# GpSimd's sums, splits and squares move to VectorE and ScalarE, and GLA's neighbour scores become products, in an encoder trunk on one core

## The chip, the core and the metric

The kernel runs on one core of a Trainium2 chip. The metric is the device time of one execution in microseconds, as the median of several runs. TensorE does the matrix products, VectorE and ScalarE the elementwise work, GpSimd some of it, and SyncE issues all DMAs.

## The reference

Two layers over 1024 tokens of 1024 features, all in float32. Each has a token mixer and a squared-ReLU MLP, with an RMS norm ahead of and behind each of them:

```python
h = x
for l in range(DEPTH):
    mixed = hybrid_mixer(rmsnorm(h, norm_pre_mix[l]), ...)   # mLSTM | GLA | retention
    h = h + rmsnorm(mixed, norm_post_mix[l])
    ff = squared_relu_mlp(rmsnorm(h, norm_pre_ffn[l]), w_ff1[l], w_ff2[l])
    h = h + rmsnorm(ff, norm_post_ffn[l])

def rmsnorm(x, g):
    return x * rsqrt(mean(x * x, axis=-1) + EPS) * g

def squared_relu_mlp(u, w1, w2):
    return square(relu(u @ w1)) @ w2
```

Gated linear attention (GLA) is one of the three mixers. Within a chunk, token i looks at token j <= i of the same head:

```python
b = cumsum(log_decay)                       # per head and feature d
scores[i, j] = sum_d q[i, d] * k[j, d] * exp(b[i, d] - b[j, d])
```

## The kernel before

The tokens are cut into two halves of 512, and a half's activations lie with features on the partitions, as 8 tiles of 128x512. A dense product is done in float32 precision by three passes (`mm3`, L268 to L270): weights and activations are split into a high part (a cast on ScalarE, `h_`/`uh_`) and the rest (a subtraction on VectorE, `l_`/`ul_`; `split`, L276 and L277). `wslot` (L257 to L264) loads and splits the weights. A group of 256 output columns (`fm_group`) has two PSUM banks, `d_...`, from a pool of two, and `evac` empties each. So a bank that is emptied late holds up the group behind it.

Beside the dense groups run generators: a mixer in quarters of 256 tokens, or a norm. `tick`, which `fm_group` calls after each block of 12 matmuls on a bank, takes the next step of them, and what a step issues stands in the program there. The framework's scheduler then sets the order on each engine, by priorities (`tc.high_priority`), and each engine works through its queue in order. All DMAs are in SyncE's queue.

The norms: `square_sum` (L345) squares 8 tiles on ScalarE (`sq_`, L353) and adds them into `ss` (L354): tiles 1 to 4 on GpSimd, 5 to 7 on VectorE. A product with a matrix of ones sums over the partitions (`nps_`), `rstd_end` makes the factor, and `pre_norm_end` (L362) scales and splits the tiles; the splits of tiles 2 and 5 are GpSimd's. `post_norm_end` (L383) does the norm behind a block: L390 multiplies by the factor and L391 applies the gain and adds the residual. There are 6 places with `square_sum`. `out_proj` (L838) copies each output tile from PSUM on ScalarE (L846), squares it and adds it to `sso`: tiles 1 to 6 on GpSimd, tile 7 on VectorE (`block_sq`, L858).

The MLP: a hidden tile is `r` = relu (ScalarE, L873), its square's high part `hi` = square(r) cast (ScalarE, L876), r*r in full (GpSimd, L877), and the rest r*r - hi (VectorE, L878). There are 128 such tiles. The second product is added up in `f` (VectorE, L897), from PSUM.

GLA's scores in `mixer`: the decay between two tokens is split at the border of a block of s tokens, for s = 64, 32, ... 1. At each of the 7 levels `level_operands` builds `Qg` and `Kg` (VectorE and an exp on ScalarE: `e`), a matrix product gives `gs`, and `copy_predicated` (L631) writes its entries, by a mask, into `Pg`. The diagonal, i = j, is a product q*k summed over each head's 32 features by a product with the selector `hsel` (`dd`), which GpSimd spreads over a diagonal (`Pg`, L619). The mixer runs 8 times.

Of the kernel before, what the change touches and what calls it, by code (L numbers as in the profile page):

```python
# [10 lines left out]
F32 = mybir.dt.float32  # L11
F32R = mybir.dt.float32r
I32 = mybir.dt.int32
U8 = mybir.dt.uint8
AF = mybir.ActivationFunctionType
ALU = mybir.AluOpType
# [3 lines left out]
P = 128  # L20
# [7 lines left out]
QT = 256  # L28
EPS = 1e-6
DFF = 4 * D  # L30
LEVELS = (64, 32, 16, 8, 4, 2, 1)
VW = 516
BIG = 1e30

# [12 lines left out]
def hybrid_trunk(ctx, tc, a, out):  # L47
# [153 lines left out]

    cb = cp.tile([P, 768], F32, tag="c_b", name="c_b")
    lmask, dm, gin = cb[:, 0:128], cb[:, 128:640], cb[:, 640:768]
    lvm = cp.tile([P, len(LEVELS) * 64], U8, tag="lvm", name="lvm")

    def load_masks():
        dma(out=cb, in_=a["c_b"])
        lvf = m1.tile([P, len(LEVELS) * 64], F32, tag="mqk", name="lvf")
        dma(out=lvf, in_=a["c_lvm"])
        V.tensor_copy(out=lvm, in_=lvf)  # L210

# [60 lines left out]
    def split(src, name, eng=V):  # L272

        hi = up.tile([P, TH], F32R, tag="uh", name=f"uh_{name}")
        lo = up.tile([P, TH], F32R, tag="ul", name=f"ul_{name}")
        S.copy(out=hi, in_=src)  # L276
        eng.tensor_tensor(out=lo, in0=src, in1=hi.bitcast(F32), op=ALU.subtract)  # L277
        return hi, lo
# [66 lines left out]
    def square_sum(tiles, name):  # L345
        ss = None
        for kt in range(KT):
            if kt == 0:
                ss = np_.tile([P, TH], F32, tag="ss", name=f"ss_{name}", bufs=3)
                S.activation(out=ss, in_=tiles[0], func=AF.Square)  # L350
            else:
                sq = np_.tile([P, TH], F32, tag="nt", name=f"sq_{name}_{kt}", bufs=3)
                S.activation(out=sq, in_=tiles[kt], func=AF.Square)  # L353
                (V if kt >= KT - 3 else G).tensor_tensor(out=ss, in0=ss, in1=sq, op=ALU.add)  # L354
        return ss

    def pre_norm(h, l, key, name):
# [4 lines left out]
    def pre_norm_end(h, r, l, key, name):  # L362
        u = []
        for kt in range(KT):
            w = np_.tile([P, TH], F32, tag="nt", name=f"w_{name}_{kt}", bufs=3)
            V.scalar_tensor_tensor(out=w, in0=h[kt], scalar=pcol(l, key, kt), in1=r, op0=ALU.mult, op1=ALU.mult)
            u.append(split(w, f"{name}_{kt}", G if kt in (2, 5) else V))
        return u

    def post_norm(half, acc, ss, l, key, name, store):  # L370
# [118 lines left out]
    def mixer(pj, prev, q):  # L489
# [117 lines left out]

        qk = m1.tile([P, QT], F32, tag="ge", name=f"qk{nm}", bufs=2)
        V.tensor_tensor(out=qk, in0=gq, in1=gk, op=ALU.mult)
        ready = level_operands(0, LEVELS[0])  # L610
        yield
        ps = psc.tile([P, 512], F32, tag="sc", name=f"dd{nm}")
        for c in range(2):
            PE.matmul(ps[:, 4 * c:4 * c + 4], qk[:, c * P:(c + 1) * P], hsel, start=True, stop=True)
        dd = m1.tile([P, 8], F32, tag="dd", name=f"dd{nm}")
        V.tensor_copy(out=dd, in_=ps[:, :8])
        Pg = m1.tile([P, 2, 4, P], F32, tag="Pg", name=f"Pg{nm}")
        Pg8 = Pg.rearrange("p c h t -> p (c h) t")
        G.tensor_tensor(out=Pg8, in0=ident.unsqueeze(1).to_broadcast([P, 8, P]), in1=dd.unsqueeze(2).to_broadcast([P, 8, P]), op=ALU.mult)  # L619
        yield  # L620
        for li, s in enumerate(LEVELS):
            qb, kb = Qg[li % 2], Kg[li % 2]
            if li + 1 < len(LEVELS):
                ready = level_operands(li + 1, LEVELS[li + 1])
            ps = psc.tile([P, 512], F32, tag="sc", name=f"gs{nm}_{s}")
            for c in range(2):
                mm = PE.matmul(ps[:, c * 256:(c + 1) * 256], kb[:, c * P:(c + 1) * P], qb[:, :, c * 64:(c + 1) * 64], start=True, stop=True)
                if c == 0 and li + 1 < len(LEVELS):
                    behind(mm, ready)
            n2 = 64 // s  # L630
            V.copy_predicated(out=Pg.rearrange("p c h (n w s) -> p (c h) n w s", w=2, s=s)[:, :, :, 1, :],  # L631
                              mask=lvm[:, li * 64:(li + 1) * 64].rearrange("p (n s) -> p n s", s=s).unsqueeze(1).to_broadcast([P, 8, n2, s]),
                              data=ps.rearrange("p (k n s) -> p k n s", k=8, s=s))
            yield
# [203 lines left out]
    def out_proj(pj, y, tiles=None):  # L838
        l, n = pj.l, pj.n
        acc = []  # L840
        ss = np_.tile([P, TH], F32, tag="ss", name=f"sso{n}", bufs=3)
        for g in range(4):
            def ev(m, ps):
                kt = 2 * g + m
                t = tiles[kt] if tiles else accp.tile([P, TH], F32, tag="acc", name=f"o{n}_{kt}")
                S.copy(out=t, in_=ps)  # L846
                acc.append(t)
                return lambda: block_sq(ss, t, tp.tile([P, TH], F32, tag="tmp", name=f"bo{n}_{kt}"), kt, G if kt < KT - 1 else V)
            fm_group(a["w_out"][l][:, 256 * g:256 * (g + 1)], y, ev, f"out{n}_{g}")
        return acc, ss  # L850

    def block_sq(ss, src, sq, kt, eng=V):

        if kt == 0:
            S.activation(out=ss, in_=src, func=AF.Square)
        else:
            S.activation(out=sq, in_=src, func=AF.Square)
            eng.tensor_tensor(out=ss, in0=ss, in1=sq, op=ALU.add)  # L858


    def ffn_steps(l, half, u, late=False, done=None):

        n = f"{l}{half}"
        st = {"acc": [None] * KT, "ss": None}
        hid = {}
        NCH = DFF // 512

        def f1(c, g):
            def ev(m, ps):
                f = 2 * g + m  # L870
                nm = f"hid{n}_{c}_{f}"
                r = tp.tile([P, TH], F32, tag="tmp", name=f"r_{nm}")
                S.activation(out=r, in_=ps, func=AF.Relu)  # L873
                hi = up.tile([P, TH], F32R, tag="uh", name=f"h_{nm}")
                lo = up.tile([P, TH], F32R, tag="ul", name=f"l_{nm}")
                S.activation(out=hi, in_=r, func=AF.Square)  # L876
                G.tensor_tensor(out=r, in0=r, in1=r, op=ALU.mult)  # L877
                V.tensor_tensor(out=lo, in0=r, in1=hi.bitcast(F32), op=ALU.subtract)  # L878
                hid[(c, f)] = (hi, lo)
            col = 512 * c + 256 * g  # L880
            fm_group(a["w_ff1"][l][:, col:col + 256], u, ev, f"f1{n}_{c}_{g}")

        def scratch(kt):
            if not late:
                return np_.tile([P, TH], F32, tag="nt", name=f"bf{n}_{kt}", bufs=3)
            return tp.tile([P, TH], F32, tag="tmp", name=f"bf{n}_{kt}")

        def f2(c, g):
            def ev(m, ps):
                kt = 2 * g + m  # L890
                if c == 0:
                    t = accp.tile([P, TH], F32, tag="acc", name=f"f{n}_{kt}")
                    V.tensor_copy(out=t, in_=ps)
                    st["acc"][kt] = t
                else:
                    t = st["acc"][kt]
                    V.tensor_tensor(out=t, in0=t, in1=ps, op=ALU.add)  # L897
                if c == NCH - 1:
                    if kt == 0:
                        st["ss"] = np_.tile([P, TH], F32, tag="ss", name=f"ssf{n}", bufs=3)  # L900
                    def rest():
                        sq = scratch(kt)
                        if done and kt == KT - 1:
                            S.activation(out=sq, in_=t, func=AF.Square)
                            st["last"] = sq
                        else:
                            block_sq(st["ss"], t, sq, kt)
                        if done:
                            done(kt, t)
                    return rest  # L910
            fm_group(a["w_ff2"][l][512 * c:512 * (c + 1), 256 * g:256 * (g + 1)], [hid[(c, f)] for f in range(4)], ev, f"f2{n}_{c}_{g}")

        steps = [lambda c=c, g=g: f1(c, g) for c in range(2) for g in range(2)]
        for c in range(NCH):
            steps += [lambda c=c, g=g: f2(c, g) for g in range(4)]
            if c + 2 < NCH:
                steps += [lambda c=c, g=g: f1(c + 2, g) for g in range(2)]
        return steps, st
# [201 lines left out]
        return done, finish  # L1120

    AFTER, NEXT = 2, 10
    PARTS = 81


    main, gates = in_groups(pj[0, 0], u0, rn0, sl0)
# [79 lines left out]
def _constants():  # L1206
# [11 lines left out]
    hsel = p[:, None] // 32 == np.arange(4)[None, :]  # L1218
    c = {"c_a": np.concatenate([np.eye(P), freq, hsel, gout], 1).astype(np.float32),
         "c_b": np.concatenate([lmask, dm.reshape(P, 4 * P), gin], 1).astype(np.float32)}  # L1220
    m = np.zeros((P, len(LEVELS), 64), np.float32)
    for li, s in enumerate(LEVELS):
        x = np.arange(64)
        blk = x // s
        m[:, li, :] = (p[:, None] // s == 2 * blk[None, :])
# [30 lines left out]
```

## Time and profile before

| | |
|---|---|
| time, median of 3 runs | 2483.89 us (2482.72 to 2485.12) |
| the profiled execution: time, span | 2483.34 us, 2481.6 us |
| TensorE busy | 2413.4 us (97%) |
| VectorE busy | 1572.0 us (63%), 2800 instructions |
| ScalarE busy | 1065.6 us (43%), 2050 instructions |
| GpSimd busy | 299.7 us (12%), 253 instructions |
| mean granted TensorE clock | 0.995 |

The span is the time from the first to the last instruction of the profiled execution; its own time is longer by what lies around it. Busy shares are means over the whole span. A wait is idle time of an engine that ended with the instruction named.

### The profile page before, as it was taken

The page shows a single profiled execution, that of the slowest core. Times are in us where ns is not written, and L with a number is a line of the kernel's source. Part 1 is how long each engine was busy: PE and PEld are TensorE (multiplying, and loading weights), DVE is VectorE, ACT ScalarE, POOL GpSimd, SP SyncE. Part 2 cuts the span into 40 slices and gives each one's busy share as a digit, 9 for nine tenths or more (in the row PEclk, how much of TensorE's full clock was granted, in tenths as well). Part 3 has the DMA queues.
Part 4 walks back from the last instruction along what each step waited for, and adds up shares of the span by engine and source line. Part 5 has one row for each costly group of instructions (what it writes and reads, how often), then busy time and mean ns, then how long its engine had stood idle before and what let it go on. Part 6 is the DMA issues. An engine that isn't in the chain of part 4 may idle for free. (4 is left out here: it accounts for less than half of the span.)

```text
span 2481.6 us, 31329 instructions
## 1 busy us (share of the span) xinstructions
PE 2413.4 (97%) x11436; PEld 1981.8 (80%) x11436; DVE 1572.0 (63%) x2800; ACT 1065.6 (43%) x2050; POOL 299.7 (12%) x253
## 2 busy tenths in 40 slices
PE   8999998999999989999999999999999999999998
PEld 7778887788788778888788878888888887888886
DVE  5888757756755685856755576776865538634434
ACT  6666344433333454633423344553433344423233
POOL 0000011101111120010110022010110012111010
PEclk9999999999999999999999999999999999999999
DMA  8645454333334355523423445543323433433331
GB/s 252 204 132 170 143 174 153 105 95 116 103 104 151 125 170 172 151 91 108 127 78 117 157 144 165 178 129 109 117 87 93 138 126 111 145 94 94 94 95 67
DMA packets 324246, 321.61 MB, mean 130 GB/s; under 512 B 15434, under 2 KB 292476, under 8 KB 324092
## 3 DMA queue, kind: packets, MB, share of 16 engines
q1 hardware_dynamic: 324092, 319.61, 41.7%
q8 instruction: 90, 1.47, 0.3%
q14 instruction: 64, 0.52, 0.1%
HBM read 263.92 MB, written 55.64 MB: 129 GB/s over the span
## 5 line engine op out<-in xcount | busy, mean ns | idle before, releaser
L263 ACT CAST h_f<-r_f 128x1024 fp32r<-128x1024 f32 x256 | 267.7, 1046 | 558.1 <-PE d_f L270 553.1
L264 DVE TENSOR_TENSOR l_f<-r_f,h_f 128x1024 fp32r<-128x1024 f32 x256 | 319.3, 1247 | 181.3 <-ACT h_f L263 178.3
L268 PE MATMUL d_f<-h_hid,l_f 128*128 128x512 f32 x1024 | 417.9, 408 | 8.6 <-DVE f L897 7.1
L268 PE MATMUL d_f<-uh_uf,l_f 128*128 128x512 f32 x1024 | 417.0, 407 | 4.3 <-ACT uh_uf L276 4.3
L269 PE MATMUL d_f<-ul_uf,h_f 128*128 128x512 f32 x1024 | 406.5, 397 | 0.1
L269 PE MATMUL d_f<-l_hid,h_f 128*128 128x512 f32 x1024 | 406.4, 397 | 0.0
L270 PE MATMUL d_f<-uh_uf,h_f 128*128 128x512 f32 x1024 | 403.3, 394 | 0.0
L270 PE MATMUL d_f<-h_hid,h_f 128*128 128x512 f32 x1024 | 402.9, 393 | 0.0
L877 POOL TENSOR_TENSOR r_hid<-r_hid 128x512 f32<-128x512 f32 x128 | 163.9, 1280 | 1127.5 <-ACT h_hid L876 1127.5
L897 DVE TENSOR_TENSOR f<-f,d_f 128x512 f32<-128x512 f32 x224 | 153.4, 685 | 140.1 <-PE d_f L270 139.6
L268 PEld LDWEIGHTS d_f<-h_hid,l_f 128*128 128x128 f32 x1024 | 193.6, 189 | 58.6 <-DVE f L897 9.4
L268 PEld LDWEIGHTS d_f<-uh_uf,l_f 128*128 128x128 f32 x1024 | 193.7, 189 | 49.7 <-ACT uh_uf L276 4.5
L270 PEld LDWEIGHTS d_f<-uh_uf,h_f 128*128 128x128 f32 x1024 | 192.8, 188 | 44.4
L270 PEld LDWEIGHTS d_f<-h_hid,h_f 128*128 128x128 f32 x1024 | 192.7, 188 | 43.9
L269 PEld LDWEIGHTS d_f<-ul_uf,h_f 128*128 128x128 f32 x1024 | 193.1, 189 | 42.2 <-issue 1.2
L269 PEld LDWEIGHTS d_f<-l_hid,h_f 128*128 128x128 f32 x1024 | 192.9, 188 | 42.5 <-issue 2.4
L878 DVE TENSOR_TENSOR l_hid<-r_hid,h_hid 128x512 fp32r<-128x512 f32 x128 | 89.4, 698 | 163.4 <-POOL r_hid L877 162.5
L264 DVE TENSOR_TENSOR l_in<-r_in,h_in 128x1024 fp32r<-128x1024 f32 (+2 forms) x96 | 122.0, 1271 | 74.4 <-ACT h_in L263 74.3
L873 ACT ACTIVATE r_hid<-d_f 128x512 f32<-128x512 f32 x128 | 76.5, 598 | 195.4 <-PE d_f L270 195.3
L263 ACT CAST h_in<-r_in 128x1024 fp32r<-128x1024 f32 (+2 forms) x96 | 101.4, 1056 | 47.7 <-PE d_in L270 39.2
L269 PE MATMUL d_in<-ul_u,h_in 128*128 128x512 f32 x256 | 101.9, 398 | 4.6 <-DVE ul_u L277 4.6
L268 PE MATMUL d_in<-uh_x,l_in 128*128 128x512 f32 x256 | 104.9, 410 | 1.1 <-DVE px L446 0.9
(394 smaller groups left out, 4261.3 us busy)
## 6 DMA issues: line engine op xcount, KB each, us to landing
r_f<-in_w_ff_dram SPq DMA_DIRECT2D x256, 512.0 KB, 3.7
r_in<-in_w_in_dram SPq DMA_DIRECT2D x80, 512.0 KB, 4.0
r_out<-in_w_out_dram SPq DMA_DIRECT2D x32, 512.0 KB, 3.5
pv<-pv SPq DMA_DIRECT2D x64, 128.0 KB, 2.4
pf<-px SPq DMA_DIRECT2D x32, 256.0 KB, 4.2
vt<-pv SPq DMA_DIRECT2D x32, 256.0 KB, 3.9
pg<-gz_g SPq DMA_DIRECT2D x32, 256.0 KB, 2.0
gt<-pg SPq DMA_DIRECT2D x32, 256.0 KB, 4.6
```

The lines of the kernel that those rows point to most:

```text
L263: S.copy(out=hi[:, :, :n], in_=raw[:, :, :n])
L264: V.tensor_tensor(out=lo[:, :, :n], in0=raw[:, :, :n], in1=hi[:, :, :n].bitcast(F32), op=ALU.subtract)
L268: nc.tensor.matmul(ps, al, bh, start=start, stop=False)
L269: nc.tensor.matmul(ps, ah, bl, start=False, stop=False)
L270: dense[0] = nc.tensor.matmul(ps, ah, bh, start=False, stop=stop)
L873: S.activation(out=r, in_=ps, func=AF.Relu)
L877: G.tensor_tensor(out=r, in0=r, in1=r, op=ALU.mult)
L878: V.tensor_tensor(out=lo, in0=r, in1=hi.bitcast(F32), op=ALU.subtract)
L897: V.tensor_tensor(out=t, in0=t, in1=ps, op=ALU.add)
```

## The change

Five things change.

1. `square_sum`: all sums are on VectorE (24 more over the 6 places).
2. `pre_norm_end`: the splits of tiles 2 and 5 are on VectorE (12 more).
3. `out_proj`: the sums of tiles 1 to 6 are on VectorE (24 more).
4. MLP: ScalarE squares `r` in place and casts it to `hi`; GpSimd has no part in it.
5. GLA: level s = 1 goes. Its entries, the score of each odd token with its left neighbour, are computed as products q*k*exp(b[i]-b[j]) in `nb` (VectorE, an exp on ScalarE), summed over a head's features by two more products with `hsel` into the tile of `dd`, and written by a `copy_predicated` over GpSimd's diagonal. One step of the generator fewer per quarter: `PARTS`, which sets the pace of the mixer, is 79 for 81.

```diff
-LEVELS = (64, 32, 16, 8, 4, 2, 1)
+LEVELS = (64, 32, 16, 8, 4, 2)
...
                 S.activation(out=sq, in_=tiles[kt], func=AF.Square)
-                (V if kt >= KT - 3 else G).tensor_tensor(out=ss, in0=ss, in1=sq, op=ALU.add)
+                V.tensor_tensor(out=ss, in0=ss, in1=sq, op=ALU.add)
...
-            u.append(split(w, f"{name}_{kt}", G if kt in (2, 5) else V))
+            u.append(split(w, f"{name}_{kt}"))
...
         V.tensor_tensor(out=qk, in0=gq, in1=gk, op=ALU.mult)
+
+        nb = m1.tile([P, QT], F32, tag="E1", name=f"nb{nm}")
+        nbv, Bp = (x.rearrange("p (n w) -> p n w", w=2) for x in (nb, B))
+        gqp, gkp = (x.rearrange("p (n w) -> p n w", w=2) for x in (gq, gk))
+        V.tensor_tensor(out=nbv[:, :, 1], in0=Bp[:, :, 1], in1=Bp[:, :, 0], op=ALU.subtract)
+        S.activation(out=nbv[:, :, 1], in_=nbv[:, :, 1], func=AF.Exp, scale=1.0 / 16.0)
+        V.tensor_tensor(out=nbv[:, :, 1], in0=gqp[:, :, 1], in1=nbv[:, :, 1], op=ALU.mult)
+        V.tensor_tensor(out=nbv[:, :, 0], in0=gkp[:, :, 0], in1=nbv[:, :, 1], op=ALU.mult)
...
             PE.matmul(ps[:, 4 * c:4 * c + 4], qk[:, c * P:(c + 1) * P], hsel, start=True, stop=True)
-        dd = m1.tile([P, 8], F32, tag="dd", name=f"dd{nm}")
-        V.tensor_copy(out=dd, in_=ps[:, :8])
+            PE.matmul(ps[:, 8 + 4 * c:12 + 4 * c], nb[:, c * P:(c + 1) * P], hsel, start=True, stop=True)
+        ddn = m1.tile([P, 16], F32, tag="dd", name=f"dd{nm}")
+        V.tensor_copy(out=ddn, in_=ps[:, :16])
+        dd = ddn[:, 0:8]
...
         yield
+        V.copy_predicated(out=Pg.rearrange("p c h (n w) -> p (c h) n w", w=2)[:, :, :, 1],
+                          mask=lvm[:, len(LEVELS) * 64:].unsqueeze(1).to_broadcast([P, 8, 64]),
+                          data=ddn[:, 8:16].unsqueeze(2).to_broadcast([P, 8, 64]))
...
-                return lambda: block_sq(ss, t, tp.tile([P, TH], F32, tag="tmp", name=f"bo{n}_{kt}"), kt, G if kt < KT - 1 else V)
+                return lambda: block_sq(ss, t, tp.tile([P, TH], F32, tag="tmp", name=f"bo{n}_{kt}"), kt)
...
-                S.activation(out=hi, in_=r, func=AF.Square)
-                G.tensor_tensor(out=r, in0=r, in1=r, op=ALU.mult)
+                S.activation(out=r, in_=r, func=AF.Square)
+                S.copy(out=hi, in_=r)
...
-    PARTS = 81
+    PARTS = 79
```

The scheduler sets the order anew, so instructions change place that the diff does not name. Three places follow, before and then after. In the names the digits after a tile's own name are layer and half (`sq_u10_4`: tile 4 of the norm ahead of layer 1, half 0). Behind line 619 the changed kernel's lines have other numbers: 846 is 859, 857 is 870, 897 is 910.

ScalarE's queue in the output projection of layer 0, half 1, with the norm ahead of layer 1 beside it. Before:

```order
L353 ACTIVATE sq_u10_5_7664<-f00_5_4815 128x512
L353 ACTIVATE sq_u10_6_7667<-f00_6_4841 128x512
L857 ACTIVATE bo01_3_7756<-o01_cv_7544 128x512
L353 ACTIVATE sq_u10_7_7670<-f00_7_4855 128x512
L263 CAST h_out01_3_1_7837<-r_out01_3_1_7835 128x4x256
L846 COPY o01_Pg_7545<-d_out01_2_0_7771 128x512
```

After:

```order
L353 ACTIVATE sq_u10_5_7644<-f00_5_4804 128x512
L353 ACTIVATE sq_u10_6_7647<-f00_6_4826 128x512
L859 COPY o01_Pg_7525<-d_out01_2_0_7751 128x512
L353 ACTIVATE sq_u10_7_7650<-f00_7_4848 128x512
L870 ACTIVATE bo01_4_7790<-o01_Pg_7525 128x512
L859 COPY o01_Pg_7525<-d_out01_2_1_7752 128x512
```

The copy of `o01_Pg` from PSUM has moved from behind the last square of the norm, `sq_u10_7`, to a place ahead of it, and the square `bo01_3` further up, out of these rows.

ScalarE's queue in the output projection of layer 0, half 0; `cv010` is the sigmoid behind the convolution of the next mixer quarter. Before:

```order
L846 COPY o00_0_3609<-d_out00_0_0_3571 128x512
L855 ACTIVATE sso00_3558<-o00_0_3609 128x512
L846 COPY o00_1_3625<-d_out00_0_1_3572 128x512
L263 CAST h_out00_2_0_3704<-r_out00_2_0_3702 128x4x256
L857 ACTIVATE bo00_1_3627<-o00_1_3625 128x512
L565 ACTIVATE cv010_4445<-mqk010_4448 128x4x256
```

After:

```order
L859 COPY o00_0_3599<-d_out00_0_0_3561 128x512
L868 ACTIVATE sso00_3548<-o00_0_3599 128x512
L565 ACTIVATE cv010_4435<-mqk010_4438 128x4x256
L859 COPY o00_1_3615<-d_out00_0_1_3562 128x512
L263 CAST h_out00_2_0_3694<-r_out00_2_0_3692 128x4x256
L870 ACTIVATE bo00_1_3617<-o00_1_3615 128x512
```

The first operation on `cv010` has moved ahead of the copy of `o00_1`.

VectorE's queue at the norm ahead of the MLP of layer 1, half 1 (`ss_uf11`), beside the MLP of half 0, whose sums are `f10_...`. Before:

```order
L897 TENSOR_TENSOR f10_2_14839<-f10_2_14839,d_f210_6_1_0_17574 128x512
L354 TENSOR_TENSOR ss_uf11_17416<-ss_uf11_17416,sq_uf11_5_17430 128x512
L354 TENSOR_TENSOR ss_uf11_17416<-ss_uf11_17416,sq_uf11_6_17433 128x512
L354 TENSOR_TENSOR ss_uf11_17416<-ss_uf11_17416,sq_uf11_7_17436 128x512
L897 TENSOR_TENSOR f10_3_14862<-f10_3_14862,d_f210_6_1_1_17575 128x512
L264 TENSOR_TENSOR l_f210_7_0_0_17730<-r_f210_7_0_0_17727,h_f210_7_0_0_17729 128x4x256
```

After:

```order
L910 TENSOR_TENSOR f10_2_14804<-f10_2_14804,d_f210_6_1_0_17534 128x512
L354 TENSOR_TENSOR ss_uf11_17376<-ss_uf11_17376,sq_uf11_1_17378 128x512
L354 TENSOR_TENSOR ss_uf11_17376<-ss_uf11_17376,sq_uf11_2_17381 128x512
L354 TENSOR_TENSOR ss_uf11_17376<-ss_uf11_17376,sq_uf11_3_17384 128x512
L910 TENSOR_TENSOR f10_3_14827<-f10_3_14827,d_f210_6_1_1_17535 128x512
L354 TENSOR_TENSOR ss_uf11_17376<-ss_uf11_17376,sq_uf11_4_17387 128x512
L264 TENSOR_TENSOR l_f210_7_0_0_17690<-r_f210_7_0_0_17687,h_f210_7_0_0_17689 128x4x256
L354 TENSOR_TENSOR ss_uf11_17376<-ss_uf11_17376,sq_uf11_5_17390 128x512
```

The sums of tiles 1 to 4, which were GpSimd's, stand behind the evacuation of `f10_2`, and those of the later tiles behind them.

## Rows read from the trace of the kernel before

**Rows 1.** Page, part 1: busy us (share of the span) and instructions of each engine.

```profile
PE 2413.4 (97%) x11436; PEld 1981.8 (80%) x11436; DVE 1572.0 (63%) x2800; ACT 1065.6 (43%) x2050; POOL 299.7 (12%) x253
```

**Rows 2.** Waits of TensorE, whole span: us in total, times, longest us.

```profile
PE d_in L269 <- DVE ul_u L277: 4.6, 4, 1.6
PE d_in L268 <- ACT gst L460: 4.4, 2, 2.2
PE gs L62 <- DVE Kg L605: 4.3, 3, 1.8
PE d_f L268 <- ACT uh_uf L276: 4.3, 1, 4.3
...
PE d_out L268 <- ACT o_Pg L846: 3.1, 2, 1.5
...
PE nps_uf L62 <- DVE ss_uf L354: 2.8, 1, 2.8
PE d_out L268 <- ACT o L846: 2.5, 1, 2.5
```

**Rows 3.** Instructions of line 391 (VectorE): duration ns min/median/max, first and last start.

```profile
L391 DVE SCALAR_TENSOR_TENSOR f<-f,prm,hl_pf_E x6: 1775/1777/1786, 861.0 to 1470.8; 128x512 f32<-128x512 f32 x6
L391 DVE SCALAR_TENSOR_TENSOR o_mqk<-o_mqk,prm,hl_pm_k x6: 743/744/747, 911.2 to 2044.4; 128x512 f32<-128x512 f32 x6
```

**Rows 4.** Timeline of VectorE, 2040 to 2062 us: start us, us, instruction, idle before.

```profile
2046.24 1.22 DVE L264 TENSOR_TENSOR l_f<-r_f,h_f 128x1024 fp32r<-128x1024 f32 x1
2047.37 1.79 DVE L391 SCALAR_TENSOR_TENSOR o_cv<-o_cv,prm,hl_pm_k 128x512 f32<-128x512 f32 x1
...
2056.59 2.28 DVE L264 TENSOR_TENSOR l_f<-r_f,h_f 128x1024 fp32r<-128x1024 f32 x1
...
2059.39 0.67 DVE L897 TENSOR_TENSOR f<-f,d_f 128x512 f32<-128x512 f32 x1
```

**Rows 5.** Timeline of TensorE, 2050 to 2062 us.

```profile
2060.12 0.79 PE L268 MATMUL d_f<-h_hid,l_f 128*128 128x512 f32 x1 [5.26 <-DVE f L897]
```

**Rows 6.** Timeline of VectorE, 388 to 428 us.

```profile
395.42 1.79 DVE L391 SCALAR_TENSOR_TENSOR o<-o,prm,hl_pm_k 128x512 f32<-128x512 f32 x1
...
404.79 2.31 DVE L264 TENSOR_TENSOR l_f<-r_f,h_f 128x1024 fp32r<-128x1024 f32 x1
```

**Rows 7.** Timeline of GpSimd, 388 to 428 us.

```profile
395.04 1.62 POOL L354 TENSOR_TENSOR ss_uf<-ss_uf,sq_uf 128x512 f32<-128x512 f32 x1 [17.39 <-ACT sq_uf L353]
...
404.48 1.55 POOL L354 TENSOR_TENSOR ss_uf<-ss_uf,sq_uf 128x512 f32<-128x512 f32 x1 [2.08 <-ACT sq_uf L353]
```

**Rows 8.** Groups of TensorE: shapes, count, busy us, mean ns, idle before.

```profile
L62 PE MATMUL gs<-Qg,Kg 128*128 128x256 f32 x224 | 57.8, 380 | 4.4 <-DVE Kg L605 4.3
...
L62 PE MATMUL dd<-c_a,qk 128*128 128x4 f32 x32 | 4.1, 235 | 2.2 <-DVE qk L609 2.2
```

**Rows 9.** Groups of GpSimd.

```profile
L877 POOL TENSOR_TENSOR r_hid<-r_hid 128x512 f32<-128x512 f32 x128 | 163.9, 1280 | 1127.5 <-ACT h_hid L876 1127.5
...
L619 POOL TENSOR_TENSOR Pg<-c_a,dd 128x1024 f32<-128x1024 f32 x8 | 16.4, 2052 | 63.7 <-DVE dd L616 43.0 <-DMA r_f<-in_w_ff_dram 20.7
```

**Rows 10.** Groups of ScalarE.

```profile
L876 ACT ACTIVATE h_hid<-r_hid 128x512 fp32r<-128x512 f32 x128 | 80.9, 632 | 1.9
```

**Rows 11.** Groups of VectorE, shapes kept apart.

```profile
L354 DVE TENSOR_TENSOR ss_uf<-ss_uf,sq_uf 128x512 f32<-128x512 f32 x12 | 8.2, 685 | 0.6 <-ACT sq_uf L353 0.3
```

**Rows 12.** Timeline of ScalarE, 336 to 356 us.

```profile
338.47 0.59 ACT L846 COPY o<-d_out 128x512 f32<-128x512 f32 x1 [1.73 <-PE d_out L270]
...
341.25 0.59 ACT L846 COPY o<-d_out 128x512 f32<-128x512 f32 x1 [1.53 <-PE d_out L270]
...
350.16 1.06 ACT L565 ACTIVATE cv<-mqk 128x1024 f32<-128x1024 f32 x1 [6.84 <-DVE mqk L562]
```

**Rows 13.** Busy time by stretch; PEclk is TensorE's granted clock, 1.00 the full one.

```profile
1531.00:1535.00 4.00, 4.00 (x20) 4.00 (x21) 2.71 (x3) 2.21 (x5) 0.00 (x0) 0.57 0.92 225
2060.00:2064.00 4.00, 3.88 (x10) 3.12 (x11) 4.00 (x7) 2.10 (x3) 0.00 (x0) 0.57 0.76 261
```

More of the change, by code (lines that the diff above doesn't have):

```diff
@@ L203, in hybrid_trunk @@
     lmask, dm, gin = cb[:, 0:128], cb[:, 128:640], cb[:, 640:768]
-    lvm = cp.tile([P, len(LEVELS) * 64], U8, tag="lvm", name="lvm")
+    lvm = cp.tile([P, len(LEVELS) * 64 + 64], U8, tag="lvm", name="lvm")
     def load_masks():
         dma(out=cb, in_=a["c_b"])
-        lvf = m1.tile([P, len(LEVELS) * 64], F32, tag="mqk", name="lvf")
+        lvf = m1.tile([P, len(LEVELS) * 64 + 64], F32, tag="mqk", name="lvf")
         dma(out=lvf, in_=a["c_lvm"])
@@ L1220, in _constants @@
          "c_b": np.concatenate([lmask, dm.reshape(P, 4 * P), gin], 1).astype(np.float32)}
-    m = np.zeros((P, len(LEVELS), 64), np.float32)
-    for li, s in enumerate(LEVELS):
+    m = np.zeros((P, len(LEVELS) + 1, 64), np.float32)
+    for li, s in enumerate(LEVELS + (1,)):
         x = np.arange(64)
```

## The prediction

> **What bounds the kernel now.** I read the busy line first: TensorE is busy 2413.4 of 2481.6 us, VectorE 63%, ScalarE 43%, GpSimd 12% [rows 1]. So TensorE's own work is the floor, and a change can save only in two ways: fewer matmuls, or shorter waits of TensorE. What is left of the span is 68 us. The view of TensorE's waits, which names the instruction that ended each, comes next [rows 2]. The waits sit in few places, not in the long MLP stretches: the first mixer (waits for `Kg`), the steps where a norm runs beside dense groups (`ul_u`, `gst`, `uh_uf`, `ss_uf`), and the evacuations of the output projection (`o_Pg`, `o` L846). In each of the norm places VectorE or ScalarE is what is waited for, and behind both stands VectorE's in-order queue. The last view is therefore the timeline of VectorE and GpSimd in those places.
>
> What the reader is to see there: L391 on 512 columns takes 743 to 747 ns in one place and 1775 to 1786 in another, with the same shape [rows 3]. The long ones lie where GpSimd runs. Near 2050 us GpSimd adds up `ss_uf` and squares `r_hid`, and in that stretch six VectorE operations with two SBUF operands are long, from L391's 1.79 us to the weight subtraction's 2.28 (1.22 elsewhere); `f` L897, which reads one operand from PSUM, keeps its 0.67 [rows 4]. Behind them `f` L897 comes late, its PSUM bank stays taken, and TensorE stands 5.26 us [rows 5]. Beside 391 to 407 us the same happens: four GpSimd sums, 1.62 to 1.55 us long [rows 7], and four long VectorE operations, 1.79 to 2.31 us [rows 6].
>
> **The change, part by part.** The sum is made against the profiled execution, 2483.34 us, which lies 0.55 under the median of the runs.
>
> *1. The GLA level that goes.* A level is 4 matmul records of `gs` (57.8 us over 56 levels: 1.03 us each); the `dd` matmuls are 4.1 us over 8 mixers, 0.51 each, and their number doubles [rows 8]. TensorE, which is nearly always busy, loses (1.03 - 0.51) x 8 = **-4.2 us**. On VectorE a level's seven small operations and its copy_predicated go, and three small ones and another copy_predicated come; that work lies beside TensorE's except in the first mixer.
>
> *2. First mixer.* Three waits for `Kg` hold 4.3 us [rows 2]; one of them goes with the level (at most -1.8, the longest). The new chain in its place is VectorE, ScalarE, VectorE, VectorE, TensorE, copy, and the copy_predicated of `ddn`, which stands behind GpSimd's `Pg` (2.05 us [rows 9]). Queued behind it on VectorE are the `Qg`/`Kg` products for which `gs` waits. At nothing hidden, that is +2.05 in each of the 8 mixers (+16); but two to six VectorE operations stand between the copy of `ddn` and this one, which cover it mostly. I take **0** here, bounds -1.8 and +4: the other seven mixers lie beside MLP groups in which TensorE waits for nothing of theirs [rows 2].
>
> *3. MLP.* GpSimd's 128 squares (1280 ns each [rows 9]) go, and with them the wait of `l_hid` for them. ScalarE now squares in place (632 ns [rows 10]) and casts: one operation more per tile, 128 x about 0.62 = +79 us on an engine that is busy 1066. Relu is what frees PSUM; blocks of 12 matmuls follow each other by 2.8 us (two copies after such blocks begin at 338.47 and 341.25 [rows 12]), while relu, square and cast, at 0.6 to 0.63 each, need about 1.9, so the extra one is hidden by the next block. I take **0**. If the cover fails, each 0.1 us exposed costs 13.
>
> *4. The norm before the MLP of the first half, 388 to 426 us.* The four long VectorE operations are 1.05, 1.04, 1.09 and 1.09 us over their usual time: 4.3 us that VectorE gets back. Four sums more enter its queue at 685 ns [rows 11], +2.7. TensorE waits here for `ss_uf` (2.8) and for `uh_uf` (4.3) [rows 2], and both stand behind this chain. With the two splits, which no longer wait for GpSimd, I take **-2.0**, bounds -6 (most of the two waits) and +2.7 (the sums alone). The Trainium skill, "SBUF — State Buffer", section "Who interferes with whom", says that a VectorE instruction with two SBUF inputs contends with a GpSimd one that reads SBUF, and that whichever comes second is blocked altogether. The trace agrees on which instructions suffer, not on how much: the 4 GpSimd sums last 6.2 us and VectorE loses 4.3 [rows 6, 7]. By the rule the term would be 1.9 larger.
>
> *5. The two output projections with norms on both sides, 848 to 933 and 1451 to 1536 us.* They are alike, and hold all of `ul_u` (4.6), `gst` (4.4) and `o_Pg` (3.1) [rows 2]: 6.0 us each. `o_Pg`'s copy stood on ScalarE behind the last square `sq_u10_7`, which waits for the last long L391; now the copy stands ahead of that square, and the L391s, 1.78 us each [rows 3], become 0.74: 1.5 us go. `ul_u` waits for GpSimd's splits; on VectorE they take about 0.69, as the sums of the same shape do [rows 11], but in the same queue: of 2.3 I leave 1.0. `gst` waits for ScalarE, held up by squares behind long VectorE operations: of 2.2 I leave 0.5. Hence -4.5 each, and 0.7 from waits in the same places that are under 0.5 each: **-10.4** for both, bounds -13.4 and 0.
>
> *6. The last half's norm, 2030 to 2062 us.* In front of the evacuation `f` L897 the long operations lose 5.9 us (1.05, 0.78, 1.09, 1.10, 0.78 and 1.06). In the new order one more L391 was moved past it and the sums all stand behind the third evacuation. The wait of 5.26 us [rows 5] falls to about nothing: **-5.2**, bounds -5.8 and -2.
>
> *7. Output projection of the first half, 330 to 362 us.* Here the order turns against the change. ScalarE's copy of `o00_1` now stands behind `cv010` L565, which needs the whole convolution of the next mixer; in the kernel before, L565 began at 350.16 after 6.84 us of waiting for it [rows 12], and the copy stood ahead of it. TensorE needs that PSUM bank by about 344.0 (the copy of `o00_0` began at 338.47, when its block had ended, and two blocks of 2.8 us lie between). The load of `cv010` stands earlier in SP's queue, ahead of two weight loads, which I put at 3 to 5 us; the copy then ends at about 347 to 349, a wait of 3 to 5 in place of the 2.5 for `o` L846 [rows 2]. I take **+2.0**, bounds 0 and +5.8 (load not earlier).
>
> *8. Small waits elsewhere*: **-0.5**.
>
> Sum: -4.2 + 0 + 0 - 2.0 - 10.4 - 5.2 + 2.0 - 0.5 = -20.3, so 2463.0, or 2463.6 on the median. One thing is not in it yet. After the longest waits TensorE's granted clock falls: it is 0.57 of full in 1531 to 1535 and in 2060 to 2064 us [rows 13], that is, for most of these it is at 1.2 GHz instead of 2.4. Each costs (1 - 0.57) x 4 = 1.7 us. If the waits before them go, 3.4 us come back; I count half. Forecast **2462 us**.
>
> **The rivals.**
> *A. Only the matmuls count.* The waits go from one instruction to another of the same queue, because VectorE gets 48 sums and 12 splits, 60 x 0.69 = 41 us, in just the norm places, for what contention cost it there. Time 2483.9 - 4.2 = 2480. For it: VectorE's queue is what is late in every one. Against: the 5.26 us wait has its long operations ahead and its new sums behind. Chance 0.09.
> *B. Slower: the sums lengthen the chain of every norm.* If the long operations are long from something other than GpSimd (the queue's DMAs, say), nothing is given back, and the six norms each gain 4 sums and 2 splits on the path: 6 x 6 x 0.69 = 24.8; less 4.2, 2504. It decides from the point where L391 stays above 1.5 us in the same places. The Trainium skill, "Perfetto Trace Analysis", section "Optimizing Scalar/DVE Operations", speaks for this side: where VectorE is saturated, work may be offloaded from it. It is at 63% over the span. Against: L391 is 0.74 wherever GpSimd rests [rows 3]. Chance 0.04.
> *C. Slower: ScalarE.* If the extra cast delays relu by 0.3 us in each of 128 tiles, +38: 2483.9 - 20 + 38 = 2502. At 43% [rows 1] and with 0.9 us free in a block it has room. Chance 0.03.
> *D. More goes:* all waits of points 4 to 6 and the slowed clock: 2483.9 - 4.2 - 7.1 - 13.4 - 5.3 - 4 = 2450. Chance 0.10.
> My case holds 0.74.
>
> **How the numbers follow.** The terms' bounds together, taken half way each, give 2455 to 2477 for the likeliest case; the range reaches to A and nearly to D: 2451 to 2480, outside which lie B, C and part of D. About 0.2% (5 us) is what a measurement of this kernel can tell from no change: faster is below 2478.9. Faster 0.84 (my case and D, with the upper tail), same 0.09 (A), slower 0.07 (B and C).
>
> **What would show it.** L391 at 0.74 us and `l_f` at 1.22 in the norm places; GpSimd's work down to `Pg` and memsets; no wait before `f` at 2060; waits for `ul_u` and `o_Pg` shorter; and a longer wait for `o` in 330 to 362 us. `gs` 192 records and `dd` 64. I am wrong if waits for `Kg` or `Pg` grow in every mixer, if TensorE begins to wait for `h_hid` or `r_hid` in the MLP stretches, or if the norm places keep their waits under other names.

## The result and the profile after

The changed kernel takes 2440.01 us (median of 3 runs, 2439.65 to 2440.81), against 2483.89: a ratio of 0.9824 with a 95% interval of 0.9802 to 0.9846. It is faster by 43.9 us, twice the 21.9 that were forecast, and below the range. Its profiled execution has a span of 2437.6 us, 44.0 less.

Where the 44.0 us lie is read first from the busy line, which answers to [rows 1]:

```profile
span 2437.6 us, 30996 instructions
PE 2399.8 (98%) x11436; PEld 1978.1 (81%) x11436; DVE 1536.9 (63%) x2828; ACT 1140.7 (47%) x2178; POOL 28.8 (1%) x65
```

TensorE is busy 13.6 us less (2413.4 before), so 30.4 us are waits that went. VectorE, which took over 60 operations, is busy 35 us less, and GpSimd nearly idle. TensorE's waits (the first is now the longest of all; the rows answer to [rows 2]):

```profile
PE d_f L268 <- ACT uh_uf L276: 6.4, 1, 6.4
...
PE gs L62 <- DVE Kg L605: 2.2, 2, 1.7
PE mn L62 <- DVE qi L705: 2.2, 1, 2.2
...
PE d_in L268 <- ACT gst L462: 0.4, 1, 0.4
...
PE nps_uf L62 <- DVE ss_uf L354: 0.3, 1, 0.3
```

The waits for `f`, `ul_u`, `o_Pg` and `o` are gone altogether, and of 4.4 us for `gst` nothing is left at its old place. The wait for `qi`, in the first mixer, is new; the GLA part alone (`e3_gla`, below) has it too. In the view of line 391 (VectorE; duration ns min/median/max, first and last start) no long operation is left; these rows answer to [rows 3]:

```profile
L391 DVE SCALAR_TENSOR_TENSOR f<-f,prm,hl_pf_E x6: 743/746/747, 847.7 to 1442.2; 128x512 f32<-128x512 f32 x6
L391 DVE SCALAR_TENSOR_TENSOR o_mqk<-o_mqk,prm,hl_pm_k x6: 745/746/748, 893.7 to 2007.0; 128x512 f32<-128x512 f32 x6
```

VectorE's timeline at the last norm, which answers to [rows 4], shows what follows: no operation is long, so `f` L910 starts at 2016.18, and TensorE doesn't wait for it.

```profile
2012.57 0.69 DVE L390 TENSOR_TENSOR o_Pg<-o_Pg,sso 128x512 f32<-128x512 f32 x1
2013.17 0.68 DVE L390 TENSOR_TENSOR o_gqk<-o_gqk,sso 128x512 f32<-128x512 f32 x1
2013.78 0.75 DVE L391 SCALAR_TENSOR_TENSOR o_Pg<-o_Pg,prm,hl_pm_E 128x512 f32<-128x512 f32 x1
2014.44 1.22 DVE L264 TENSOR_TENSOR l_f<-r_f,h_f 128x1024 fp32r<-128x1024 f32 x1
2015.58 0.69 DVE L891 TENSOR_TENSOR l_hid<-r_hid,h_hid 128x512 fp32r<-128x512 f32 x1
2016.18 0.68 DVE L910 TENSOR_TENSOR f<-f,d_f 128x512 f32<-128x512 f32 x1
```

In the stretches by time, the granted clock (the number before the last two) is full where it was 0.57 of full behind the long waits [rows 13]: that work lies in the second and third rows. It still falls around the one long wait that is left, which ends at 416 us, and now also behind the wait for `qi`, which ends at 266 us. The columns are PE, PEld, DVE, ACT and POOL busy, PEclk, DMA share and GB/s:

```profile
836.00:913.00 77.00, 76.77 (x390) 64.23 (x388) 65.27 (x91) 45.72 (x80) 0.21 (x2) 1.00 0.60 188
1428.00:1505.00 77.00, 76.89 (x390) 64.39 (x389) 65.25 (x91) 45.68 (x80) 0.21 (x2) 1.00 0.61 195
2016.00:2020.00 4.00, 4.00 (x19) 3.22 (x18) 4.00 (x7) 1.05 (x1) 0.00 (x0) 1.00 0.59 202
411.00:420.00 9.00, 3.69 (x8) 2.48 (x9) 9.00 (x16) 4.52 (x10) 0.00 (x0) 0.62 0.46 131
266.00:270.00 4.00, 4.00 (x13) 3.17 (x12) 2.42 (x11) 0.39 (x2) 0.00 (x0) 0.57 0.33 98
```

The first two hold the work that took 848 to 933 and 1451 to 1536 us before: 77 us for 85, with TensorE hardly waiting.

The matmuls that start the norms' sums over the partitions serve as marks that both kernels have. First and last start of two of them, in the kernel before:

```profile
L62 PE MATMUL nps_pf<-ssf,ones x6: 590/594/595, 847.8 to 2111.6; 128*128 128x512 f32 x6
L62 PE MATMUL nps_pm<-sso,ones x8: 590/592/595, 385.5 to 2034.0; 128*128 128x512 f32 x8
```

and after:

```profile
L62 PE MATMUL nps_pf<-ssf,ones x6: 590/594/595, 835.5 to 2067.8; 128*128 128x512 f32 x6
L62 PE MATMUL nps_pm<-sso,ones x8: 590/592/595, 382.2 to 1998.0; 128*128 128x512 f32 x8
```

So 3.3 us are won by the first mark, 12.3 by 848 us, 36.0 by 2034 and 43.8 by 2112, and nothing behind it. With the starts of the same dense matmul in both traces, the gain divides so (us; the forecast's terms are put to the stretches in which they lay, the 0.52 of a level in each mixer):

| stretch of the kernel before | forecast | measured | of it waits |
|---|---|---|---|
| to 359: input, first mixer, first output projection | +1.0 | -3.3 | -3.8 |
| 359 to 459: first norm ahead of the MLP | -2.0 | -5.1 | -2.1 |
| the six mixer quarters beside MLP groups | -3.6 | -10.7 | -5.8 |
| 858 to 987 and 1462 to 1591: norms and input projection | -10.4 | -17.1 | -12.8 |
| 2042 to 2090: last norm | -5.2 | -7.8 | -5.8 |
| clock regained | -1.7 | within the rows above | |

### The profile page after: what moved, and what is told of

It reads as the page before. It is cut to its first block, busy times and chain, and to the rows that moved or that the text cites. A ratio compares the mean times of both kernels' runs of the same rounds, so it can differ in the third digit from the quotient of the medians.

```text
span 2437.6 us, 30996 instructions
## 1 busy us (share of the span) xinstructions
PE 2399.8 (98%) x11436; PEld 1978.1 (81%) x11436; DVE 1536.9 (63%) x2828; ACT 1140.7 (47%) x2178; POOL 28.8 (1%) x65
## 4 chain that ended last, share of the span: by engine, by line
PE 88%; DVE 6%; DMA 2%; issue 1%; ACT 1%; SPq 0%; DVEq 0%; ACTq 0%
PE d_f L269 19%; PE d_f L268 19%; PE d_f L270 19%; PE d_in L269 5%; PE d_in L268 5%; PE d_in L270 5%; PE d_out L269 2%; PE d_out L268 2%; PE d_out L270 2%; PE gr L62 2%; PE gs L62 1%; PE mn L62 1%; DVE l_in L264 1%; PE mu L62 1%; PE gu L62 1%
## 5 line engine op out<-in xcount | busy, mean ns | idle before, releaser
L910 DVE TENSOR_TENSOR f<-f,d_f 128x512 f32<-128x512 f32 x224 | 153.5, 685 | 159.8 <-PE d_f L270 159.1
L269 PEld LDWEIGHTS d_f<-ul_uf,h_f 128*128 128x128 f32 x1024 | 192.7, 188 | 42.6 <-issue 1.7
L891 DVE TENSOR_TENSOR l_hid<-r_hid,h_hid 128x512 fp32r<-128x512 f32 x128 | 88.3, 690 | 91.4 <-ACT h_hid L890 90.8
L269 PE MATMUL d_in<-ul_x,h_in 128*128 128x512 f32 x256 | 102.1, 399 | 0.0
L270 PE MATMUL d_in<-uh_x,h_in 128*128 128x512 f32 x256 | 102.0, 398 | 0.0
```

The source lines that it names most:

```text
L269: nc.tensor.matmul(ps, ah, bl, start=False, stop=False)
L270: dense[0] = nc.tensor.matmul(ps, ah, bh, start=False, stop=stop)
```

## The experiments

Theory 1: GpSimd's tensor operations make VectorE's operations with two SBUF operands longer, VectorE's queue falls behind, and TensorE waits; the gain is what that cost. Its rivals: the gain comes from the new order of the queues (and from waits for GpSimd's own results), or from the GLA part. The ratio and interval are those to the kernel before on the same chip; the last column is the difference to the median of the kernel named, before on the same chip, and 2440.01 us for the changed kernel.

| kernel | median us | ratio, 95% interval | against |
|---|---|---|---|
| e1_norms: norms' edits alone | 2456.44 | 0.9896, 0.9879 to 0.9912 | before -27.2 |
| e2_mlp: MLP's edit alone | 2473.10 | 0.9962, 0.9947 to 0.9977 | before -10.6 |
| e3_gla: GLA's edit alone | 2478.82 | 0.9981, 0.9970 to 0.9991 | before -4.8 |
| e4_gpsimd: norms and MLP | 2444.97 | 0.9849, 0.9834 to 0.9864 | before -38.7 |
| e5_read: changed, with idle reads on GpSimd | 2469.61 | 0.9937, 0.9923 to 0.9952 | changed +29.6 |
| e6_write: changed, with idle memsets | 2439.17 | 0.9823, 0.9805 to 0.9841 | changed -0.8 |
| e7_read_mlp: idle reads at the MLP only | 2447.44 | 0.9852, 0.9837 to 0.9866 | changed +7.4 |
| e8_cover: changed, one more group beside a norm | 2432.15 | 0.9788, 0.9772 to 0.9804 | changed -7.9 |
| e10_changed: the changed kernel | 2441.54 | 0.9823, 0.9806 to 0.9839 | |
| e9_no_gpsimd: e8 and the diagonal on ScalarE | 2430.62 | 0.9777, 0.9762 to 0.9791 | e10 -10.9 |

**The parts alone.** `e1_norms` has the three edits of `square_sum`, `pre_norm_end` and `out_proj`, `e2_mlp` that of the MLP, `e4_gpsimd` all four, `e3_gla` the rest of the change:

```diff
# e1_norms, from the kernel before
-                (V if kt >= KT - 3 else G).tensor_tensor(out=ss, in0=ss, in1=sq, op=ALU.add)
+                V.tensor_tensor(out=ss, in0=ss, in1=sq, op=ALU.add)
-            u.append(split(w, f"{name}_{kt}", G if kt in (2, 5) else V))
+            u.append(split(w, f"{name}_{kt}"))
-                return lambda: block_sq(ss, t, tp.tile(...), kt, G if kt < KT - 1 else V)
+                return lambda: block_sq(ss, t, tp.tile(...), kt)
# e2_mlp, from the kernel before
-                S.activation(out=hi, in_=r, func=AF.Square)
-                G.tensor_tensor(out=r, in0=r, in1=r, op=ALU.mult)
+                S.activation(out=r, in_=r, func=AF.Square)
+                S.copy(out=hi, in_=r)
```

Expected of `e1_norms`:

> The kernel before with the three edits of the norms alone (sums and splits of square_sum, pre_norm_end and out_proj on VectorE); GpSimd still squares in the MLP and the seventh GLA level stays. The changed kernel gained 43.9 us. Theory 1 (GpSimd's tensor operations stretch VectorE's two-operand ones): the norm places at 388 to 459, 848 to 941 and 1451 to 1545 us gain nearly all that they gained in the changed kernel (4.6 + 8.0 + 8.7), the last one (7.8) part of it since GpSimd's MLP squares still run there: 2455 to 2462 us, L391 at 0.74 in the first three. Theory 2 (the new order of the queues gains, not the speed of VectorE's operations; VectorE pays 41 us more work): 2475 to 2490. Theory 3 (most of it is the GLA part): 2475 to 2484.

Of `e2_mlp`:

> The kernel before with the edit of the MLP alone (ScalarE squares in place and casts, GpSimd doesn't square); GpSimd keeps its sums and splits in the norms. Theory 1: the MLP stretches beside a mixer lose the waits that lie there (some 6 us over three mixers), the norm at 2030 to 2062 us gains part of its 7.8, the other norm places nothing: 2470 to 2478 us. Theory 2: 2480 to 2490, since ScalarE gets 79 us of work. Theory 3: 2480 to 2484.

Of `e3_gla`:

> The kernel before with the edit of the GLA scores alone (six levels, neighbours by products; PARTS 79); GpSimd works as before. Theory 1: only TensorE's own time counts, the groups gs and dd being 2.7 us shorter together in the changed kernel, and a wait or two in the first mixer: 2477 to 2482 us. Theory 3: the mixers' stretches gave 14 us in the changed kernel, and all of it comes from this part: 2467 to 2473.

Of `e4_gpsimd`:

> The kernel before with all four edits that free GpSimd, and the seventh GLA level kept. Theory 1: what the GLA part adds is TensorE's 2.7 us and a few tenths of waits: 2441 to 2446 us. Theory 2: no statement beyond the sum of the two parts alone. Theory 3: 2452 to 2458, the rest being the GLA part's.

The three parts add up: 27.2 + 10.6 + 4.8 = 42.6, of 43.9; the two of GpSimd 37.8, of 38.7 together. Theory 3 falls. In `e1_norms` the two stretches with norms on both sides (858 to 987 and 1462 to 1591 us) gain 8.2 and 8.9 us, all that they gained in the changed kernel, and line 391 is short there, while `f` L897 is still waited for beside the MLP's squares on GpSimd, which stay in this kernel:

```profile
L391 DVE SCALAR_TENSOR_TENSOR f<-f,prm,hl_pf_E x6: 740/744/749, 853.8 to 1450.3; 128x512 f32<-128x512 f32 x6
```

```profile
PE d_f L268 <- DVE f L897: 4.3, 6, 2.0
```

In `e2_mlp` it is the other way round. The waits of the norm places stand as in [rows 2] and line 391 is long, but the waits in the mixers beside the MLP have shrunk (from 2.0, 1.7 and 2.6 us in the three pairs of quarters to 0, 1.1 and 1.1), and at the last norm 2.1 of the 5.3 us are left:

```profile
L391 DVE SCALAR_TENSOR_TENSOR f<-f,prm,hl_pf_E x6: 1775/1778/1786, 855.4 to 1465.4; 128x512 f32<-128x512 f32 x6
```

```profile
PE d_in L269 <- DVE ul_u L277: 4.6, 4, 1.6
...
PE d_f L268 <- DVE f L897: 2.1, 1, 2.1
```

These runs don't yet tell theory 1 from the order, since taking the work off GpSimd also sets the queues anew, and takes away results that VectorE's queue waited for.

**GpSimd busy for nothing.** The next three put work back on GpSimd of which nobody takes a result, in the changed kernel, with the same order of instructions on TensorE, VectorE, ScalarE and SyncE:

```diff
# e5_read, from the changed kernel; called where GpSimd worked in the kernel before
+    lfa = cp.tile([P, QT], F32, tag="lfa", name="lfa")
+    da = lfa[64:128, :]
...
+    def load_gpsimd(cause):
+        for k in range(2):
+            i = G.tensor_tensor(out=da, in0=da, in1=da, op=ALU.mult)
+            if k == 0:
+                after(i, cause)
...
-                S.activation(out=r, in_=r, func=AF.Square)
+                load_gpsimd(S.activation(out=r, in_=r, func=AF.Square))
# e6_write: instead of the two products
+        for k in range(4):
+            i = G.memset(da, 0.0)
```

(`lfa` takes the place of the tile `lf`, whose upper partitions are free.) Expected of `e5_read`:

> The changed kernel with idle work put back on GpSimd: wherever GpSimd worked in the kernel before (sums and splits of the norms, sums of the output projection, squares of the MLP), it multiplies a small tile with itself twice (64 partitions x 256, from SBUF to SBUF, about 1.3 us), as soon as ScalarE has made the value that GpSimd used to take. Nobody reads the result, and the order of the instructions on TensorE, VectorE, ScalarE and SyncE is that of the changed kernel. Theory 1 (GpSimd's operations stretch VectorE's): L391 and the other two-operand ones go back to 1.5 to 1.8 us in the norm places, and the time to 2465 to 2485 us, since VectorE now has the sums as well. Rival (the gain is from the new order and from waits for GpSimd's results): 2438 to 2443, as nobody waits for GpSimd.

Of `e6_write`:

> As the run before it, but GpSimd's idle work is four memsets of the same tile, which write SBUF and read nothing, in the same places. If it is GpSimd's reading that stretches VectorE's operations: 2438 to 2444 us, L391 at 0.74. If any work of GpSimd does: 2460 to 2485. Rival (order): 2438 to 2443, too; so this run tells only together with the one before.

Of `e7_read_mlp`:

> The changed kernel with the reading idle work of GpSimd at the MLP's 128 squares alone. Theory 1: the MLP edit alone gained 10.5 us in the kernel before, so about that much is lost: 2446 to 2455 us, with waits in the MLP stretches beside a mixer and before the evacuation of f at about 2016 us. Rival (order): 2438 to 2443.

With the reads the kernel loses 29.6 us, with the memsets nothing that its four runs (2437.43 to 2446.19) can tell. The rival predicted 2438 to 2443 for both. GpSimd's busy groups in `e5_read` and in `e6_write`, first one, then the other:

```profile
L323 POOL TENSOR_TENSOR lfa<-lfa 64x256 f32<-64x256 f32 x376 | 377.3, 1003 | 1459.3 <-ACT r_hid L907 1045.9 <-ACT sq_u L365 120.0 <-ACT bo L886 106.8
```

```profile
L323 POOL MEMSET lfa<- 64x256 f32 x752 | 231.3, 308 | 1563.5 <-ACT r_hid L907 1096.0 <-ACT sq_u L365 123.6 <-ACT bo L886 115.6
```

and VectorE's line with the residual (391 in the other kernels) in `e5_read` and in `e6_write`:

```profile
L407 DVE SCALAR_TENSOR_TENSOR f<-f,prm,hl_pf_E x6: 1098/1100/1107, 850.7 to 1455.7; 128x512 f32<-128x512 f32 x6
```

```profile
L407 DVE SCALAR_TENSOR_TENSOR f<-f,prm,hl_pf_E x6: 743/746/750, 849.1 to 1443.4; 128x512 f32<-128x512 f32 x6
```

The operation is 0.35 us longer beside the reads and not at all beside the memsets, which run beside it as often: of this line's 56 operations of that shape 24 overlap a read, and 23 of them take 0.93 us or more; 23 overlap a memset, and none takes over 0.76. That it was expected at 1.5 to 1.8 us is a miss of size: the idle operation has half the columns, and half the partitions, of the real one. The Trainium skill, "SBUF — State Buffer", section "Who interferes with whom", says that such a VectorE instruction contends with a GpSimd one that reads SBUF and not with one that only writes it: `e5_read` and `e6_write` agree. That the second to issue is blocked altogether fits the rows as well. GpSimd's idle products near 2035 us, then VectorE's operations there:

```profile
2031.30 2.50 POOL L323 TENSOR_TENSOR lfa<-lfa 64x256 f32<-64x256 f32 x1 [8.22 <-ACT sq_uf L365]
...
2035.93 0.94 POOL L323 TENSOR_TENSOR lfa<-lfa 64x256 f32<-64x256 f32 x1
2036.95 0.94 POOL L323 TENSOR_TENSOR lfa<-lfa 64x256 f32<-64x256 f32 x1
```

```profile
2032.04 0.68 DVE L406 TENSOR_TENSOR o_cv<-o_cv,sso 128x512 f32<-128x512 f32 x1
2032.64 0.69 DVE L406 TENSOR_TENSOR o_Pg<-o_Pg,sso 128x512 f32<-128x512 f32 x1
2033.24 1.11 DVE L407 SCALAR_TENSOR_TENSOR o_cv<-o_cv,prm,hl_pm_E 128x512 f32<-128x512 f32 x1
...
2035.30 1.10 DVE L909 TENSOR_TENSOR l_hid<-r_hid,h_hid 128x512 fp32r<-128x512 f32 x1
2036.32 1.10 DVE L406 TENSOR_TENSOR o_Pg<-o_Pg,sso 128x512 f32<-128x512 f32 x1
2037.35 1.10 DVE L406 TENSOR_TENSOR o_gqk<-o_gqk,sso 128x512 f32<-128x512 f32 x1
...
2041.13 0.67 DVE L928 TENSOR_TENSOR f<-f,d_f 128x512 f32<-128x512 f32 x1
```

The two engines take turns. `l_hid` ends at 2036.40, the product beside it 0.47 us later, at 2036.87; `o_Pg` ends 0.55 behind that, at 2037.42, and the next product 0.47 behind `o_Pg`. The first product, which finds VectorE at work, takes 2.50 us: two VectorE operations run beside it at their usual length, and it ends 0.47 us behind the second.

This is the changed kernel's own queue, with the same operations in front of `f` (L928 here) as in the rows after. Six operations in front of `f` are long, and TensorE waits 1.2 us for it. With the idle work at the MLP's squares alone, `e7_read_mlp`, the loss is 7.4 us, and the stretches in which it lies are those where `e2_mlp` gained: +3.0, +0.6 and +2.1 us in the mixers beside the MLP, +1.8 at the last norm.

The idle work takes back 29.6 of the 38.7 us of `e4_gpsimd`, and at the MLP alone 7.4 of the 10.6 of `e2_mlp`. The idle operations are smaller than the real ones, so less was to be expected; but a part of the rest can be the results that VectorE no longer waits for. Its `l_hid` sat idle for GpSimd's `r_hid` 102 times before, 162.5 us in all, and sits idle for ScalarE's `h_hid` 49 times after, 90.8 us, in `e7_read_mlp` just as long. No run separates the two causes.

**What is left.** `e8_cover` sets one group of the second half's input projection behind the first output projection, so that the norm's chain has more dense work beside it:

```diff
-    run(main[:4])
+    run(main[:3])
     flush(m)
     y = load_y(pj[0, 0])
-    run(main[4:5])
+    run(main[3:4])
...
-    run(main[5:])
+    run(main[4:])
```

(and the first mixer's pace goes from 1.75 to 2.1). Expected:

> The changed kernel with one more group of the second half's input projection behind the first output projection, beside the norm that follows it (and so the first mixer is flushed one group earlier, at a pace of 2.1 steps for 1.75). The changed kernel's longest wait, 6.4 us for uh_uf at 416 us, and the slowed clock behind it should go, up to 8 us; the earlier flush of the mixer may cost 1 to 4. 2432 to 2440 us; if the wait is bound by the chain of the norm and not by the work beside it, 2440 to 2443.

The wait of 6.4 us for `uh_uf` is gone and the slowed clock behind it, 6.0 us less in that stretch, and the kernel is at 2432 us. The stretch in the columns of above:

```profile
405.00:420.00 15.00, 14.94 (x94) 12.96 (x94) 14.07 (x22) 9.67 (x16) 0.00 (x0) 1.00 0.58 185
```

The longest waits that it leaves in the whole span:

```profile
PE gs L62 <- DVE Kg L605: 4.5, 4, 1.8
PE pps L65 <- DMA pre_row<-in_norm_pre_mix_dram: 3.0, 1, 3.0
PE dd L62 <- DVE qk L609: 2.6, 1, 2.6
```

All three are before 316 us. Then the last tensor operation of GpSimd went, beside the changed kernel once more:

```diff
-        G.tensor_tensor(out=Pg8, in0=ident..., in1=dd..., op=ALU.mult)
+        for k in range(8):
+            S.mul(out=Pg8[:, k, :], in_=ident, mul=dd[:, k:k + 1])
```

> The changed kernel itself, so that the next kernel is compared with it on one chip, and to see how far the stretch up to 316 us, where no two of the kernels agree to better than 2 us, differs between two executions of the same instructions. 2438 to 2443 us; if that stretch differs by 1 us or more here as well, differences of that size there are no effect of an edit.

> The kernel with one more group beside the first norm (2432 us), and GLA's diagonal, GpSimd's last tensor operation (8 times 2.1 us), made by ScalarE in 8 scaled copies of 128x128 each. Theory 1 (stretched VectorE operations cost time only where TensorE waits behind them): in the mixers beside the MLP TensorE no longer waits, so only the first mixer can gain: 2430 to 2433 us. If every stretch of a VectorE operation costs time, some 8 us: 2422 to 2426.

At 2430.6 us `e9_no_gpsimd` is the fastest kernel of the study, 10.9 below the changed kernel on its chip. Its step from `e8_cover`, 1.5 us, is within what theory 1 gave and can't be told from no change. That the operations stretched by `Pg` cost little agrees with it: in the mixers beside the MLP no matmul waits behind them. Of the first mixer, where some do, the repeat below allows no reading.

The repeat of the changed kernel shows how much of a difference at the start is none. The same mark as above:

```profile
L62 PE MATMUL nps_pm<-sso,ones x8: 590/592/595, 384.2 to 2000.3; 128*128 128x512 f32 x8
```

It is 2.0 us later by the first norm and 2.3 by the last. Between executions of the same instructions, then, some 2 us lie in the first 382 us, and a difference of that size in that stretch isn't put down to an edit here.

## Why the prediction was wrong

The mechanism was right and the direction too: `e5_read` and `e6_write` show that GpSimd's reads made VectorE's operations long, and the waits went where they were named. What failed is the size, step by step:

- **3, the MLP, "I take 0".** This is the step that failed most: by the table the mixers beside the MLP gave 7.1 us more than forecast, the largest miss of a row. I asked only whether ScalarE's extra cast would be hidden (it is: in `e2_mlp` and after TensorE waits next to nothing for `r_hid`), and gave the 128 squares that leave GpSimd no term except the one at the last norm. Alone they are worth 10.6 us, of which 3.4 lie at the last norm, and reading work put back in their place costs 7.4. The rest lies mostly in the mixers beside the MLP, where waits of 0.2 to 1.1 us behind VectorE's queue add up: before, 1.96, 1.69 and 2.58 us in the three pairs of mixer quarters, after, 0.14, 0 and 0.34. I had put down 0.5 for all small waits of the span.
- **5, the two projections, -10.4.** Measured -17.1. The waits went to 0.3 us of 13.1, so all that I left over for `ul_u` and `gst` was wrong: once VectorE's chain is ahead nothing in it is late. The rest, 4.3, is TensorE's own time on the same matmuls. A part is the slowed clock of 1531 to 1535 us [rows 13], counted in half. Another is a cost of each wait that I had not in the sum: by the starts of the same matmuls, eight of the waits (two each for `o_cv`, `o_Pg`, `ul_u` and `gst`) cost 0.26 to 0.33 us each beyond their length, since the first two matmuls behind them start further apart than after the change.
- **6, the last norm, -5.2.** The waits of the stretch went whole, -5.8 (5.26 of it the one computed), and 2.0 came on top, most of it the slowed clock (1.7, counted in half), which is full there now.
- **4, the first norm, -2.0.** Measured -5.1; the wait for `uh_uf` grew to 6.4 us, that for `ss_uf` went (2.8 to 0.3), and the clock's fall is shorter: on the mean 0.86 of full over 405 to 429 us, where it was 0.79 over 408 to 432. I had left the clock out of this term. `e3_gla` alone left this stretch at -0.5, `e1_norms` at -3.2.
- **7, the first output projection, +2.0.** Wrong in sign. ScalarE's order is as read, `cv` L565 ahead of the copy, but not 3 to 5 us were won by the earlier load of `cv010`: the convolution, which had waited for it, began 8.1 us earlier, at 333.99 instead of 342.06. L565 began at 341.18, and the copy behind it, at 342.14, was in time.

```profile
341.18 1.06 ACT L565 ACTIVATE cv<-mqk 128x1024 f32<-128x1024 f32 x1 [2.02 <-DVE mqk L562]
342.14 0.57 ACT L859 COPY o<-d_out 128x512 f32<-128x512 f32 x1
```

- **1, the level, -4.2.** `gs` went from 57.8 us to 50.2, nearly as counted (7.6 of 8.2). The small products don't cost what the group's mean said: each of the two groups of `dd` is now 5.4 to 5.7 us long, where I had 4.1. Busy times of neighbours overlap; by the starts of the matmuls the level and the products together gave 2.7 us. The part alone (`e3_gla`) gave 4.8, with an interval of 2.2 to 7.5. What it gave beyond TensorE's 2.7 lies, in its profiled execution, ahead of 359 us: the wait of 2.5 us for `o` is gone there (2.4 of it stand in `e4_gpsimd`), but that is a stretch in which executions of the same instructions differ by some 2 us.
- **2, the first mixer, 0.** -1.7 up to 316 us, no more than a repeat differs by (2.6 there).

Two readings of the rows were wrong and left the sum as it was. Under 4 I set 6.2 us of GpSimd's sums against 4.3 that VectorE lost and took the 1.9 between them as a difference to the rule named there. But the sums' durations hold GpSimd's own waiting for VectorE (last section), so they are not what VectorE should lose. And `f` L897 in [rows 4], at 2059.39, doesn't show that a PSUM operand spares it: GpSimd's last sum there had ended at 2057.79. Elsewhere four of its 224 operations overlap one of GpSimd's, and take 0.68 to 0.69 us.

Of the rivals, D (all waits and the clock) was nearest; it gave 2450, since it, too, had nothing for the mixers beside the MLP. A, B and C are out: line 391 is at 0.75 us, and no wait names the extra cast.

## What to carry to other kernels

Where GpSimd and VectorE both work on SBUF tiles, an operation that is given to GpSimd and reads SBUF isn't free even if nobody waits for its result: compare the duration of one VectorE line where GpSimd runs and where it rests, and price the difference over all VectorE operations that meet it, in every stretch, not just at the long waits. Small waits in many places behind one engine's queue are one term, and when that engine gets ahead they go together. A long wait of TensorE is to be priced with the slowed matmuls behind it, read from the granted clock of that stretch. And idle work on an engine, with the order of all others kept, tells contention from order in one pair of runs.

## What the runs showed of the hardware

GpSimd waits as well. Its idle product of 64x256 at the MLP's squares in `e7_read_mlp` (duration ns min/median/max) takes 0.61 us at the shortest and 0.94 or 0.95 in turns with VectorE, as in the rows above:

```profile
L321 POOL TENSOR_TENSOR lfa<-lfa x256: 610/945/2767, 428.3 to 2387.4; 64x256 f32<-64x256 f32 x128
```

What VectorE loses is set by where GpSimd's operation ends, not by its own length. In the kernel before, 45 VectorE operations of 512 columns begin while a GpSimd one runs and take over 0.85 us: all of them end 0.54 to 0.55 us behind that one, whether it is a sum or a square; in `e5_read` 133 do, all at 0.55. [rows 6] and [rows 7] have a case of each size: the sum that starts at 395.04 ends at 396.66 and L391 at 397.21; the one that starts at 404.48 ends at 406.03 and the weight subtraction, with 1024 columns, at 407.10. So the loss is about 1.05 us beside sums of 512 columns, both for L391 with 512 columns [rows 3] and for the weight subtraction with 1024 (2.28 for 1.22 [rows 4]), 0.78 beside the MLP's squares of 512 columns (L391 at 2049.09 takes 1.52), and 0.35 to 0.42 in turns with the products of 256. The durations of both engines, where they meet, hold the time in which one waits for the other: added up, they count it twice.
